# Loading slabs 2-3 in two halves of 64 partitions, slabs 4-5 in one piece, and the tables as 16 rows: a rotary embedding kernel

## The chip, the cores and the metric

The kernel runs on one core of a Trainium2 chip. The metric is the device time of one execution in microseconds. A core has TensorE (PE, matrix products), VectorE (DVE), ScalarE (ACT), GpSimd (POOL) and SyncE (SP), which run their own instruction streams and wait for one another by semaphores, and 16 DMA engines, which move data between the memory outside (HBM) and the core's own memory of 128 partitions. DMAs are issued here from SP (all loads of `x`) and from ACT (the tables and all stores), so there are two DMA queues, and every DMA engine has a ring of packets for each.

## The reference

```
x: [16, 512, 1024] f32, seen as [batch, seq, 16 heads, 64]; cos, sin: [512, 32] f32
x1, x2 = x[..., :32], x[..., 32:]
out = concatenate([x1 * cos - x2 * sin, x1 * sin + x2 * cos], axis=-1)
```

`cos` and `sin` depend on the place in the sequence alone: they are shared by all batches and heads. The input and the output have 33.55 MB each, the two tables 64 KB each.

## The kernel before, in words

The batch is cut into eight *slabs* of two batches (4.19 MB each). In a slab each of the 128 partitions holds 8 rows of 1024 numbers, 32 KB in one piece of HBM. Slabs 2-3 and 4-5 are *pairs*: there a partition holds 16 rows in sequence, 64 KB in one piece, and the first eight of them are called slab 2 or 4, the last eight slab 3 or 5. So a partition of a pair needs other rows of the tables than one of a single slab, and there are two sets of tables: `tab` for slabs 0, 1, 6, 7 and `tab2` for 2 to 5.

Loads are issued by SP in the order of the slabs, all at the start but for the last two: slab 0 and slab 1 (line 68), slabs 2-3 as one DMA of 128 packets of 64 KB (line 87), slabs 4 and 5 as two DMAs of 128 packets of 32 KB (line 90). The loads of slabs 6 and 7 take the memory of slabs 0 and 1 and wait until these are stored (line 68 again).

Work on a slab goes through ACT, DVE and ACT. ACT casts f32 to bf16 (`cast`, line 157), into the lower half of the slab's own memory. DVE makes two products with the tables (line 175) and a sum of one with the other shifted by half a head (line 176). ACT casts back to f32 (line 179) and issues the store. Slabs 0, 6 and 7 go through in two passes of 4096 columns, the others in one of 8192. The cast of the next pass is written ahead of the products of this one; within that, a scheduler fixes each engine's order when the kernel is built, and on the chip each engine keeps to it. Slabs 4 and 5 are stored by one DMA, the others by one each.

The tables are built at the start. `cos` and `sin` are loaded as 64 partitions of 1 KB (line 83), POOL casts them to bf16 (line 116), and PE spreads them over 128 partitions by products with 0/1/-1 matrices that POOL prepares (lines 94 to 109): four matmuls for `tab` (line 121, copied out of PSUM by DVE, line 127) and eight for `tab2` (line 133, copied by ACT, line 172). DVE's first product of slab 0 waits for `tab`.

Of the kernel before, what the change touches and what calls it, by code (L numbers as in the profile page):

```python
# [9 lines left out]
@with_exitstack  # L10
def kernel(
    ctx: ExitStack,
    tc: tile.TileContext,
    x: bass.AP,
    cos: bass.AP,
    sin: bass.AP,
    num_heads: int,
    out: bass.AP,
):
    nc = tc.nc  # L20
    P = nc.NUM_PARTITIONS

    batch, seq, dim = x.shape
    nh = num_heads
    hd = dim // nh
    half = hd // 2
    bf16 = mybir.dt.bfloat16
    f32 = mybir.dt.float32

    nb = 2  # L30
    nslabs = batch // nb
    rpp = nb * seq // P
    W = rpp * dim
    SP = seq // rpp
    TW = rpp * half

    out_flat = out.rearrange("b s h d -> b s (h d)")

    singles = ctx.enter_context(tc.tile_pool(name="singles", bufs=1))
    slabs = ctx.enter_context(tc.tile_pool(name="slabs", bufs=2))  # L40
    pairs = ctx.enter_context(tc.tile_pool(name="pairs", bufs=2))
    psum = ctx.enter_context(tc.tile_pool(
        name="psum", bufs=1, space=bass.MemoryType.PSUM))


    def dram(t, s, a=0, n=W):
        return bass.AP(tensor=t.tensor, offset=t.offset + s * nb * seq * dim + a,
                       ap=[[W, P], [1, n]])


    def view(t, offset, *dims):
        return dataclasses.replace(t, offset=t.offset + offset,
                                   ap=[t.ap[0], *[list(d) for d in dims]])

    slab = {}


    def paired(t, s, a=0, n=2 * W):
        return bass.AP(tensor=t.tensor, offset=t.offset + s * nb * seq * dim + a,
                       ap=[[2 * W, P], [1, n]])


    def load(s):
        slab[s] = slabs.tile([P, W], f32, tag="slab", name="slab")
        nc.sync.dma_start(out=slab[s], in_=dram(x, s))  # L68


    def place(s):
        t = pairs.tile([P, 2 * W], f32, tag="pair", name="pair")
        slab[s], slab[s + 1] = view(t, 0, (1, W)), view(t, W, (1, W))
        return t


    load(0)


    cos_sb = singles.tile([SP, TW], f32, tag="cos_sb")  # L80
    sin_sb = singles.tile([SP, TW], f32, tag="sin_sb")
    for t, src in ((cos_sb, cos), (sin_sb, sin)):
        nc.scalar.dma_start(out=t, in_=bass.AP(
            tensor=src.tensor, offset=src.offset, ap=[[TW, SP], [1, TW]]))

    load(1)
    nc.sync.dma_start(out=place(2), in_=paired(x, 2))
    pair = place(4)
    for h in range(2):
        nc.sync.dma_start(out=slab[4 + h], in_=paired(x, 4, h * W, W))  # L90


    pick = singles.tile([SP, 2 * P], bf16, tag="pick")
    nc.gpsimd.memset(pick, 0.0)  # L94
    for g in range(2):
        part = view(pick, g * P, (SP, P // SP), (1, SP))
        nc.gpsimd.affine_select(  # L97
            out=part, in_=part, compare_op=mybir.AluOpType.not_equal,
            fill=1.0 - 2.0 * g, base=0, pattern=[[0, P // SP], [-1, SP]],
            channel_multiplier=1)  # L100

    pick2 = singles.tile([SP, 4 * P], bf16, tag="pick2")
    nc.gpsimd.memset(pick2, 0.0)  # L105
    for h in range(2):
        for g in range(2):
            part = view(pick2, (2 * h + g) * P, (SP // 2, 2 * P // SP), (1, SP // 2))
            nc.gpsimd.affine_select(  # L109
                out=part, in_=part, compare_op=mybir.AluOpType.not_equal,  # L110
                fill=1.0 - 2.0 * g, base=-h, pattern=[[0, 2 * P // SP], [-2, SP // 2]],
                channel_multiplier=1)

    tab1 = singles.tile([SP, 2 * TW], bf16, tag="tab1")
    for i, t in enumerate((cos_sb, sin_sb)):
        nc.gpsimd.tensor_copy(out=view(tab1, i * TW, (1, TW)), in_=t)  # L116

    acc = psum.tile([P, 2 * rpp * hd], f32, tag="acc")
    for i in range(2):
        for h in range(2):  # L120
            nc.tensor.matmul(  # L121
                view(acc, i * rpp * hd + h * half, (hd, rpp), (1, half)),
                view(pick, i * h * P, (1, P)),
                view(tab1, i * TW, (half, rpp), (1, half)),
                start=True, stop=True)
    tab = singles.tile([P, 2 * rpp * hd], bf16, tag="tab")
    nc.vector.tensor_copy(out=tab, in_=acc)  # L127

    acc2 = psum.tile([P, 4 * rpp * hd], f32, tag="acc2")
    for i in range(2):  # L130
        for r in range(2):
            for h in range(2):
                nc.tensor.matmul(  # L133
                    view(acc2, (2 * i + r) * rpp * hd + h * half, (hd, rpp), (1, half)),
                    view(pick2, (2 * r + i * h) * P, (1, P)),
                    view(tab1, i * TW, (half, rpp), (1, half)),
                    start=True, stop=True)
    tab2 = singles.tile([P, 4 * rpp * hd], bf16, tag="tab2")

    passes = []
    for s in range(nslabs):
        n = rpp if 1 <= s < nslabs - 2 else rpp // 2
        passes += [(s, r, n) for r in range(0, rpp, n)]


    def halves(u):
        s, r, n = u  # L150
        t = view(slab[s], 0, (1, W)).bitcast(bf16)
        return [view(t, (2 * r + i * n) * dim, (1, n * dim)) for i in range(2)]


    def cast(u):
        s, r, n = u
        nc.scalar.copy(out=halves(u)[0], in_=view(slab[s], r * dim, (1, n * dim)))  # L157


    def factor(u, i):  # L160
        s, r, n = u
        t, a = (tab2, (2 * i + s % 2) * rpp * hd) if 2 <= s < 6 else (tab, i * rpp * hd)
        return view(t, a + r * hd, (hd, n), (0, nh), (1, hd))


    cast(passes[0])
    for i, u in enumerate(passes):
        s, r, n = u
        if i + 1 < len(passes):
            cast(passes[i + 1])  # L170
        if i == 0:
            tc.keep_in_program_order(nc.scalar.copy(out=tab2, in_=acc2))  # L172
        lo, up = halves(u)
        for k, t in enumerate((up, lo)):
            nc.vector.tensor_mul(out=t, in0=lo, in1=factor(u, k))  # L175
        nc.vector.tensor_add(  # L176
            out=up, in0=up, in1=view(lo, half, (hd, n * nh), (-half, 2), (1, half)))

        nc.scalar.copy(out=view(slab[s], r * dim, (1, n * dim)), in_=up)  # L179
        if r + n == rpp:  # L180
            if s == 5:
                nc.scalar.dma_start(out=paired(out_flat, 4), in_=pair)
            elif s in (2, 3):
                nc.scalar.dma_start(out=paired(out_flat, 2, (s - 2) * W, W), in_=slab[s])
            elif s != 4:
                nc.scalar.dma_start(out=dram(out_flat, s), in_=slab[s])
            if s < 2:
                load(s + 6)

# [34 lines left out]
```

## Time and profile before

| | |
|---|---|
| runs | 166.65 us median of 3 (164.38 to 167.47) |
| the profiled execution | 161.82 us, of which the span from first to last instruction is 160.0 us |
| DVE busy | 108.4 us (68%) |
| ACT busy | 115.1 us (72%) |
| PE, POOL busy | 2.9 and 3.3 us |
| DMA | 67.24 MB, mean 420 GB/s; packets 2176 |
| cosine, sine | landed 11.6 and 16.4 us after their issue |

The durations in the text come from the profiled execution, which is quicker than the median of the runs. A line of a table of groups or of the timeline names the source line, the engine, the operation, and the tiles written and read. Busy digits stand for slices of a fortieth of the span, 9 for 90% or more.

### The profile page before, as it was taken

To read this page: it belongs to the slowest core of one execution; us is meant where nothing else is said; L and a number is where in the kernel's file an instruction comes from. 1 tells how busy PE (TensorE), PEld (TensorE's weight loads), DVE (VectorE), ACT (ScalarE), POOL (GpSimd) and SP (SyncE) were. 2 spreads that over 40 slices of the span, in tenths; PEclk is the share of its full clock that TensorE was granted. 3 is DMA by queue.
4 is the path that set the end of the run, shared out by engine and by line. 5 is a ranking of instruction groups with operands and counts; after the bars stand their busy time and mean duration, and the time that the engine had idled before them with its cause. 6 is when DMAs were issued, how large, how long until landed. Compare 5 with 4: busy or idle time off the path is not lost.

```text
span 160.0 us, 179 instructions
## 1 busy us (share of the span) xinstructions
PE 2.9 (2%) x12; PEld 1.6 (1%) x12; DVE 108.4 (68%) x34; ACT 115.1 (72%) x24; POOL 3.3 (2%) x14
## 2 busy tenths in 40 slices
PE   0001410000000000000000000000000000000000
PEld 0000300000000000000000000000000000000000
DVE  0000299999971999899899989999279399910000
ACT  3005979994099999999999999399993999380000
POOL 6000000000000000000000000000000000000000
DMA  7999999699699999999999999999998998999994
GB/s 246 410 410 410 393 524 491 295 524 491 295 393 491 426 393 442 459 410 418 459 434 393 475 442 393 450 459 401 442 491 377 524 410 377 393 459 459 393 450 205
DMA packets 2176, 67.24 MB, mean 420 GB/s; under 512 B 256, under 2 KB 384, under 8 KB 384
## 3 DMA queue, kind: packets, MB, share of 16 engines
q1 hardware_dynamic: 1008, 33.55, 49.3%
q10 hardware_dynamic: 1168, 33.69, 48.8%
HBM read 33.69 MB, written 33.55 MB: 420 GB/s over the span
## 4 chain that ended last, share of the span: by engine, by line
DMA 67%; ACT 13%; issue 5%; DVE 4%; SPq 1%; ACTq 0%
DMA pair<-in_x_dram 27%; DMA slab<-in_x_dram 26%; DMA out_dram<-slab 15%; ACT slab L179 9%; DVE slab L175 3%; ACT slab L157 3%; ACT pair L157 2%; DVE slab L176 1%; SPq L68 1%; ACTq L179 0%; ACTq L157 0%
## 5 line engine op out<-in xcount | busy, mean ns | idle before, releaser
L175 DVE TENSOR_TENSOR slab<-slab,tab 128x4096 bf16<-128x4096 bf16 (+1 forms) x14 | 36.2, 2594 | 7.0 <-ACT slab L157 6.6
L157 ACT CAST slab<-slab 128x4096 bf16<-128x4096 f32 (+1 forms) x7 | 28.5, 4090 | 17.0 <-DMA slab<-in_x_dram 17.0
L175 DVE TENSOR_TENSOR pair<-pair,tab 128x8192 bf16<-128x8192 bf16 x8 | 35.4, 4424 | 6.2 <-ACT pair L157 6.0
L157 ACT CAST pair<-pair 128x8192 bf16<-128x8192 f32 x4 | 28.1, 7015 | 6.6 <-DMA pair<-in_x_dram 6.6
L179 ACT CAST slab<-slab 128x4096 f32<-128x4096 bf16 (+1 forms) x7 | 28.5, 4090 | 3.5 <-DVE slab L176 3.5
L179 ACT CAST pair<-pair 128x8192 f32<-128x8192 bf16 x4 | 28.1, 7016 | 0.3 <-DVE pair L176 0.3
L176 DVE TENSOR_TENSOR slab<-slab 128x4096 bf16<-128x4096 bf16 (+1 forms) x7 | 18.2, 2596 | 0.2
L176 DVE TENSOR_TENSOR pair<-pair 128x8192 bf16<-128x8192 bf16 x4 | 17.7, 4425 | 0.1
L127 DVE CAST tab<-acc 128x1024 bf16<-128x1024 f32 x1 | 1.2, 1224 | 18.8 <-PE acc L121 18.8
L157 ACT ACT_TABLE_LOAD x1 | 1.3, 1283 | 2.0 <-issue 2.0
L133 PE MATMUL acc<-tab,pick 64*128 64x256 bf16 x8 | 1.9, 414 | 0.0
L172 ACT CAST tab<-acc 128x2048 bf16<-128x2048 f32 x1 | 1.9, 1857 | 0.0
L121 PE MATMUL acc<-tab,pick 64*128 64x256 bf16 x4 | 1.2, 392 | 17.6 <-POOL tab L116 17.6
L133 PEld LDWEIGHTS <-pick 64*128 64x128 bf16 x8 | 1.1, 143 | 0.6
L109 POOL TENSOR_SCALAR_AFFINE_SELECT pick<-pick 64x128 bf16<-64x128 bf16 x4 | 1.1, 301 | 0.0
L121 PEld LDWEIGHTS <-pick 64*128 64x128 bf16 x4 | 0.5, 112 | 17.8 <-issue 15.9
L116 POOL CAST tab<-cos_sb 64x256 bf16<-64x256 f32 x1 | 0.4, 389 | 9.3 <-DMA cos_sb<-in_cos_dram 9.3
L97 POOL TENSOR_SCALAR_AFFINE_SELECT pick<-pick 64x128 bf16<-64x128 bf16 x2 | 0.5, 287 | 0.0
L105 POOL MEMSET pick<- 64x512 bf16 x1 | 0.5, 522 | 0.0
L116 POOL CAST tab<-sin_sb 64x256 bf16<-64x256 f32 x1 | 0.4, 394 | 4.9 <-DMA sin_sb<-in_sin_dram 4.9
L94 POOL MEMSET pick<- 64x256 bf16 x1 | 0.3, 304 | 0.3 <-POOLq L205 0.3
L205 POOL MEMSET const-bfloat16-1.0<- 128x1 bf16 x1 | 0.1, 111 | 0.0
(3 smaller groups left out, 0.3 us busy)
## 6 DMA issues: line engine op xcount, KB each, us to landing
slab<-in_x_dram SPq DMA_DIRECT2D x4, 4096.0 KB, 31.9
out_dram<-slab ACTq DMA_DIRECT2D x4, 4096.0 KB, 21.4
pair<-in_x_dram SPq DMA_DIRECT2D x2, 4096.0 KB, 71.0
out_dram<-pair ACTq DMA_DIRECT2D x2, 4096.0 KB, 31.8
cos_sb<-in_cos_dram ACTq DMA_DIRECT2D x1, 64.0 KB, 11.6
sin_sb<-in_sin_dram ACTq DMA_DIRECT2D x1, 64.0 KB, 16.4
pair<-in_x_dram SPq DMA_DIRECT2D x1, 42.7
out_dram<-pair ACTq DMA_DIRECT2D x1, 26.4
```

The costliest lines, as they stand in the source:

```text
L68: nc.sync.dma_start(out=slab[s], in_=dram(x, s))
L97: nc.gpsimd.affine_select(out=part, in_=part, compare_op=mybir.AluOpType.not_equal, fill=1.0 - 2.0 * g, base=0, pattern=[[0, P // SP], [-1 ...
L109: nc.gpsimd.affine_select(out=part, in_=part, compare_op=mybir.AluOpType.not_equal, fill=1.0 - 2.0 * g, base=-h, pattern=[[0, 2 * P // SP] ...
L116: nc.gpsimd.tensor_copy(out=view(tab1, i * TW, (1, TW)), in_=t)
L121: nc.tensor.matmul(view(acc, i * rpp * hd + h * half, (hd, rpp), (1, half)), view(pick, i * h * P, (1, P)), view(tab1, i * TW, (half, rpp) ...
L127: nc.vector.tensor_copy(out=tab, in_=acc)
L133: nc.tensor.matmul(view(acc2, (2 * i + r) * rpp * hd + h * half, (hd, rpp), (1, half)), view(pick2, (2 * r + i * h) * P, (1, P)), view(tab ...
L157: nc.scalar.copy(out=halves(u)[0], in_=view(slab[s], r * dim, (1, n * dim)))
L172: tc.keep_in_program_order(nc.scalar.copy(out=tab2, in_=acc2))
L175: nc.vector.tensor_mul(out=t, in0=lo, in1=factor(u, k))
L176: nc.vector.tensor_add(out=up, in0=up, in1=view(lo, half, (hd, n * nh), (-half, 2), (1, half)))
L179: nc.scalar.copy(out=view(slab[s], r * dim, (1, n * dim)), in_=up)
```

## The change

All pairs of slabs (0-1, 2-3, 4-5, 6-7) get the layout of 64 KB to a partition. Three pair tiles replace two slab tiles and two pair tiles; slabs 6-7 take the place of 0-1. Slabs 0, 1, 6 and 7 are still loaded and stored one by one, in packets of 32 KB. The tables are then the same for all pairs, and differ between even and odd slabs (`tabs[s % 2]`). `cos` and `sin` are loaded as 16 rows of 4 KB each into one tile of 128 partitions, which DVE sets to zero first, cosine at partitions 0, 8, 16, ..., sine at 4, 12, 20, ...; the matrices pick the rows, in pairs of accumulating matmuls.

```diff
-    slabs = ctx.enter_context(tc.tile_pool(name="slabs", bufs=2))
-    pairs = ctx.enter_context(tc.tile_pool(name="pairs", bufs=2))
+    pairs = ctx.enter_context(tc.tile_pool(name="pairs", bufs=3))
...
+    places = [pairs.tile([P, 2 * W], f32, tag="pair", name="pair") for _ in range(3)]
+    def here(s, n=1):
+        return view(places[s // 2 % 3], s % 2 * W, (1, n * W))
+    def there(t, s, n=1):
+        return bass.AP(tensor=t.tensor, offset=t.offset + s // 2 * 2 * P * W + s % 2 * W,
+                       ap=[[2 * W, P], [1, n * W]])
+    def load(s, n=1):
+        nc.sync.dma_start(out=here(s, n), in_=there(x, s, n))
+    def store(s, n=1):
+        nc.scalar.dma_start(out=there(out_flat, s, n), in_=here(s, n))
...
-    load(0)
-    cos_sb = singles.tile([SP, TW], f32, tag="cos_sb")
-    sin_sb = singles.tile([SP, TW], f32, tag="sin_sb")
-    for t, src in ((cos_sb, cos), (sin_sb, sin)):
-        nc.scalar.dma_start(out=t, in_=bass.AP(
-            tensor=src.tensor, offset=src.offset, ap=[[TW, SP], [1, TW]]))
-    load(1)
-    nc.sync.dma_start(out=place(2), in_=paired(x, 2))
-    pair = place(4)
-    for h in range(2):
-        nc.sync.dma_start(out=slab[4 + h], in_=paired(x, 4, h * W, W))
+    TR = 16
+    TC = seq * half // TR
+    raw = singles.tile([P, TC], f32, tag="raw")
+    nc.vector.memset(raw, 0.0)
+    load(0)
+    for i, src in enumerate((cos, sin)):
+        to = dataclasses.replace(
+            raw, offset=raw.offset + 4 * i * raw.ap[0][0],
+            ap=[[P // TR * raw.ap[0][0], TR], [1, TC]])
+        nc.scalar.dma_start(out=to, in_=bass.AP(
+            tensor=src.tensor, offset=src.offset, ap=[[TC, TR], [1, TC]]))
+    load(1)
+    for p in range(0, P, P // 2):
+        part = slice(p, p + P // 2)
+        nc.sync.dma_start(out=here(2, 2)[part], in_=there(x, 2, 2)[part])
+    load(4, 2)
...
+    pick = singles.tile([P, 6 * P], bf16, tag="pick")
+    nc.gpsimd.memset(pick, 0.0)
+    for g in range(3):
+        for m in range(2):
+            part = view(pick, (g * 2 + m) * P + m, (2 * TR, P // TR // 2), (2, TR))
             nc.gpsimd.affine_select(
                 out=part, in_=part, compare_op=mybir.AluOpType.not_equal,
+                fill=-1.0 if g == 2 else 1.0, base=-4 if g else 0,
+                pattern=[[0, P // TR // 2], [-(P // TR), TR]], channel_multiplier=1)
...
+    raw_b = singles.tile([P, TC], bf16, tag="raw_b")
+    nc.gpsimd.tensor_copy(out=raw_b, in_=raw)
+    accs, tabs = [], []
+    for h in range(2):
+        acc = psum.tile([P, 2 * rpp * hd], f32, tag=f"acc{h}", name="acc")
+        for g, at in ((0, 0), (0, half), (1, rpp * hd), (2, rpp * hd + half)):
+            for m in range(2):
+                nc.tensor.matmul(
+                    view(acc, at, (hd, rpp), (1, half)),
+                    view(pick, (g * 2 + m) * P, (1, P)),
+                    view(raw_b, (2 * m + h) * TW, (half, rpp), (1, half)),
+                    start=m == 0, stop=m == 1)
...
+    nc.vector.tensor_copy(out=tabs[0], in_=accs[0])
...
-            tc.keep_in_program_order(nc.scalar.copy(out=tab2, in_=acc2))
+            tc.keep_in_program_order(nc.scalar.copy(out=tabs[1], in_=accs[1]))
...
             if s == 5:
-                nc.scalar.dma_start(out=paired(out_flat, 4), in_=pair)
-            elif s in (2, 3):
-                nc.scalar.dma_start(out=paired(out_flat, 2, (s - 2) * W, W), in_=slab[s])
+                store(4, 2)
             elif s != 4:
-                nc.scalar.dma_start(out=dram(out_flat, s), in_=slab[s])
+                store(s)
```

The passes themselves are unchanged in the source. The order that the scheduler fixes for ACT and DVE is another one around slabs 1 to 3 (casts in are called "in", casts back "back"; DVE's two products of a slab are m and its sum a):

```
ACT before: ... 0 back, store 0, 2 in, 1 back, 3 in, store 1, 2 back, 4 in, store 2, 3 back, ...
ACT after:  ... 0 back, store 0, 1 back, store 1, 2 in, 3 in, 2 back, 4 in, store 2, 3 back, ...
DVE before: ... 1m 1m 1a, 2m 2m 2a, 3m 3m 3a, 4m ...
DVE after:  ... 1m 1m 1a, 2m 2m, 3m, 2a, 3m 3a, 4m ...
```

SP's order is that of the slabs in both. The load of slabs 4-5 now waits on the semaphore of load 0 before it is issued; the loads of slabs 6 and 7 wait for stores 0 and 1 as before.

More of the change, by code (lines that the diff above doesn't have):

```diff
@@ L33 @@
     W = rpp * dim
-    SP = seq // rpp
     TW = rpp * half
@@ L39 @@
     singles = ctx.enter_context(tc.tile_pool(name="singles", bufs=1))
-    slabs = ctx.enter_context(tc.tile_pool(name="slabs", bufs=2))
-    pairs = ctx.enter_context(tc.tile_pool(name="pairs", bufs=2))
+    pairs = ctx.enter_context(tc.tile_pool(name="pairs", bufs=3))
     psum = ctx.enter_context(tc.tile_pool(
         name="psum", bufs=1, space=bass.MemoryType.PSUM))
-    def dram(t, s, a=0, n=W):
-        return bass.AP(tensor=t.tensor, offset=t.offset + s * nb * seq * dim + a,
-                       ap=[[W, P], [1, n]])
     def view(t, offset, *dims):
@@ L53, in view @@
                                    ap=[t.ap[0], *[list(d) for d in dims]])
[L58 to L74, printed above, removed]
@@ L77 @@
-    load(0)
-    cos_sb = singles.tile([SP, TW], f32, tag="cos_sb")
-    sin_sb = singles.tile([SP, TW], f32, tag="sin_sb")
-    for t, src in ((cos_sb, cos), (sin_sb, sin)):
-        nc.scalar.dma_start(out=t, in_=bass.AP(
-            tensor=src.tensor, offset=src.offset, ap=[[TW, SP], [1, TW]]))
-    load(1)
-    nc.sync.dma_start(out=place(2), in_=paired(x, 2))
-    pair = place(4)
-    for h in range(2):
-        nc.sync.dma_start(out=slab[4 + h], in_=paired(x, 4, h * W, W))
-    pick = singles.tile([SP, 2 * P], bf16, tag="pick")
@@ L94 @@
-    nc.gpsimd.memset(pick, 0.0)
[L95 to L108, printed above, removed]
+    places = [pairs.tile([P, 2 * W], f32, tag="pair", name="pair") for _ in range(3)]
@@ L109 @@
+    load(4, 2)
+    pick = singles.tile([P, 6 * P], bf16, tag="pick")
+    nc.gpsimd.memset(pick, 0.0)
+    for g in range(3):
+        for m in range(2):
+            part = view(pick, (g * 2 + m) * P + m, (2 * TR, P // TR // 2), (2, TR))
             nc.gpsimd.affine_select(
                 out=part, in_=part, compare_op=mybir.AluOpType.not_equal,
-                fill=1.0 - 2.0 * g, base=-h, pattern=[[0, 2 * P // SP], [-2, SP // 2]],
-                channel_multiplier=1)
-    tab1 = singles.tile([SP, 2 * TW], bf16, tag="tab1")
@@ L115 @@
[L115 to L132, printed above, removed]
-                nc.tensor.matmul(
[L134 to L138, printed above, removed]
+                fill=-1.0 if g == 2 else 1.0, base=-4 if g else 0,
@@ new lines @@
+                pattern=[[0, P // TR // 2], [-(P // TR), TR]], channel_multiplier=1)
[6 more added lines that the diff above has]
+            for m in range(2):
+                nc.tensor.matmul(
+                    view(acc, at, (hd, rpp), (1, half)),
+                    view(pick, (g * 2 + m) * P, (1, P)),
+                    view(raw_b, (2 * m + h) * TW, (half, rpp), (1, half)),
+                    start=m == 0, stop=m == 1)
+        accs.append(acc)
+        tabs.append(singles.tile([P, 2 * rpp * hd], bf16, tag=f"tab{h}", name="tab"))
@@ L150, in halves @@
         s, r, n = u
-        t = view(slab[s], 0, (1, W)).bitcast(bf16)
+        t = here(s).bitcast(bf16)
         return [view(t, (2 * r + i * n) * dim, (1, n * dim)) for i in range(2)]
@@ L156, in cast @@
         s, r, n = u
[L157 to L163, printed above, removed]
+        nc.scalar.copy(out=halves(u)[0], in_=view(here(s), r * dim, (1, n * dim)))
     cast(passes[0])
@@ L171 @@
         if i == 0:
-            tc.keep_in_program_order(nc.scalar.copy(out=tab2, in_=acc2))
+            tc.keep_in_program_order(nc.scalar.copy(out=tabs[1], in_=accs[1]))
         lo, up = halves(u)
-        for k, t in enumerate((up, lo)):
-            nc.vector.tensor_mul(out=t, in0=lo, in1=factor(u, k))
+        for t, a in ((up, 0), (lo, rpp * hd)):
+            nc.vector.tensor_mul(
+                out=t, in0=lo,
+                in1=view(tabs[s % 2], a + r * hd, (hd, n), (0, nh), (1, hd)))
         nc.vector.tensor_add(
             out=up, in0=up, in1=view(lo, half, (hd, n * nh), (-half, 2), (1, half)))
-        nc.scalar.copy(out=view(slab[s], r * dim, (1, n * dim)), in_=up)
+        nc.scalar.copy(out=view(here(s), r * dim, (1, n * dim)), in_=up)
         if r + n == rpp:
             if s == 5:
-                nc.scalar.dma_start(out=paired(out_flat, 4), in_=pair)
-            elif s in (2, 3):
-                nc.scalar.dma_start(out=paired(out_flat, 2, (s - 2) * W, W), in_=slab[s])
+                store(4, 2)
             elif s != 4:
-                nc.scalar.dma_start(out=dram(out_flat, s), in_=slab[s])
+                store(s)
             if s < 2:
```

## The prediction

> **What bounds the kernel now.** I read the page's slices first, then the DMA share by stage, the timeline, the DMA view by window.
>
> ```profile
> span 160.0 us, 179 instructions
> ...
> DVE  0000299999971999899899989999279399910000
> ACT  3005979994099999999999999399993999380000
> ...
> DMA  7999999699699999999999999999998998999994
> ```
>
> The DMA row is full nearly throughout (a packet counts where it starts, hence some 6s). ScalarE (ACT) has a hole in the tenth and eleventh slices, VectorE (DVE) in the thirteenth, and both stand idle in the last four. The windows view gives share and rate by stage (columns: busy time per engine, clock, DMA share, GB/s):
>
> ```profile
> 22.00:42.00 20.00, 0.00 (x0) 0.00 (x0) 19.90 (x8) 14.75 (x4) 0.00 (x0) 1.00 0.98 423
> 44.00:118.00 74.00, 0.00 (x0) 0.00 (x0) 63.85 (x17) 70.67 (x12) 0.00 (x0) 1.00 1.00 432
> 120.00:138.00 18.00, 0.00 (x0) 0.00 (x0) 14.97 (x7) 14.66 (x5) 0.00 (x0) 1.00 1.00 433
> 140.00:157.00 17.00, 0.00 (x0) 0.00 (x0) 0.69 (x1) 3.60 (x1) 0.00 (x0) 1.00 1.01 436
> ```
>
> Loads alone (22 to 42), loads with stores, stores alone: about 432 GB/s each time. All 67.2 MB at that rate are 155.6 us of the 160.0. So the DMA engines are the bound, and compute only has to hand over the stores early enough. How much room it has, the timeline tells (start, duration, what, idle before it):
>
> ```profile
> 37.86 0.35 ACTq L186 DMA_DIRECT2D out_dram<-slab  x1
> 42.51 4.42 DVE L176 TENSOR_TENSOR slab<-slab 128x8192 bf16<-128x8192 bf16 x1
> 44.40 7.02 ACT L157 CAST pair<-pair 128x8192 bf16<-128x8192 f32 x1 [6.57 <-DMA pair<-in_x_dram]
> 51.33 7.01 ACT L179 CAST slab<-slab 128x8192 f32<-128x8192 bf16 x1
> 51.45 8.88 DVE L175 TENSOR_TENSOR pair<-pair,tab 128x8192 bf16<-128x8192 bf16 x2 [4.52 <-ACT pair L157]
> ...
> 113.45 0.34 ACTq L182 DMA_DIRECT2D out_dram<-pair  x1
> ...
> 144.41 0.34 ACTq L186 DMA_DIRECT2D out_dram<-slab  x1
> ```
>
> ACT takes slab 2's cast in as soon as it has landed (44.40), and only then casts slab 1 back (51.33). The last store is issued at 144.41, 15.6 us before the end, though 4.19 MB at 432 GB/s are 9.7 us: it queues behind earlier stores for 15.6 - 9.7 - 1.0 (issue to first packet) - 1.2 (last packet to the end) = 3.7 us. Compute that comes up to 3.7 us later costs nothing; beyond that each microsecond counts.
>
> **The change, part by part.**
>
> *64 KB descriptors for slabs 4-5.* The DMA view of three windows (6 to 16, 16 to 22, 124 to 136; packets, MB, share of 16 engines):
>
> ```profile
> q1 hardware_dynamic: 143, 4.16, 101.2%
> ...
> q1 hardware_dynamic: 79, 2.59, 100.2%
> ...
> q10 hardware_dynamic: 80, 5.24, 100.8%
> ```
>
> 79 packets of 32 KB in 6 us: 6 x 16 x 1.002 / 79 = 1.22 us each. 80 of 64 KB in 12 us: 12 x 16 x 1.008 / 80 = 2.42 us. Two small ones are 2.44, so 128 large for 256 small save 128 x 0.02 / 16 = 0.16 us in all. Packets of two queues take turns on an engine: cosine's four rounds of 1 KB need 11.6 us to land beside the loads. A 64 KB load packet against a 32 KB store packet then takes two thirds of the engine, so slabs 4-5 need 8 x (2.42 + 1.22) = 29 us and land at about 72. Slab 4 is wanted later than that (below, at C + 31.8). SP now waits for load 0 to land (13.3) before issuing this load; its ring then still holds the loads of slabs 1 to 3, so nothing runs dry.
>
> *Tables.* In the window from 6 to 16 us 127 load packets took 10 x 16 x 1.012 / 127 = 1.275 us instead of 1.22, because the 1 KB table packets land between them: 127 x 0.057 = 7.2 us, and 6.1 us of their own (3.8% of 10 x 16 us), so 13.3 / 16 = 0.8 us of DMA time. With 32 packets of the same bytes it is between a quarter of that and all of it: a gain of 0 to 0.6. Instead of five turns per table (four packets and a completion) there are two. Cosine is issued later, after a DVE memset of 128x1024 (not in the trace; between 0 and the 1.22 us of the 128x1024 copy out of PSUM; I take 1.2). First packets came at 6.0, so now 7.2; four turns of 1.3 make 12.4, and 0.5 until a waiting engine starts 12.9. POOL's cast of 128x1024: between 0.39 (the 64x256 row, if columns cost nothing) and 4 x 0.39 = 1.56; I take 1.4, to 14.3. Eight matmuls (eight took 1.91): 2.0, to 16.3. The copy to the table 1.2, to 17.5, as slab 0's first cast ends (17.4). DVE starts slab 0 at 17.5 instead of 20.13. POOL's longer memset and six selects lie under the 12 us of waiting; table 1's copy on ACT is 1.0 us instead of 1.86, in a hole before load 1 lands. If the tables came as late as before, everything below moves by 2.6.
>
> *The order on ACT and DVE.* This is what I price at most. ACT casts slab 1 back, issues store 1, and only then casts slab 2; DVE does slab 3's first multiply ahead of slab 2's add. DVE: slab 0 takes 6 x 2.29, slab 1 3 x 4.43, so 17.5 + 13.7 + 13.3 = 44.5. ACT casts slab 1 back from 44.5 to 51.5, having stood idle from 37.9. Slab 2's cast starts at C = 51.5, not 44.4, if slab 2 has landed. DVE is idle until C + 7.0.
>
> From C by program order, with 7.0 for an 8192 cast, 3.6 for a 4096 cast, 4.43 and 2.29 on DVE: slab 2's add is fourth on DVE and ends at C + 24.7; slab 2 back to C + 31.8, slab 4's cast to 38.9, slab 3 back to 45.9, slab 5's cast to 52.9; slab 5 on DVE from there to 66.2, back to 73.3, store 4-5 issued at C + 73.4 (before: 113.45 - 44.40 = 69.1). The four half passes then alternate ACT and DVE: store 6 at C + 87.6, store 7 at C + 101.7 (before: 100.0). So store 7 goes from 144.4 to 153.2, 8.8 later, against 3.7 of room. The end: store 4-5 finds the queue empty (store 2 is issued at C + 31.9 and store 3 at C + 46.0, 9.7 us of transfer each, so the engines stand idle before it), so C + 73.4 + 1.0 + 19.4 + 9.7 + 9.7 + 1.2 = C + 114.4 = 166 us. That is +6 without any price for the split.
>
> *Slabs 2-3 as two loads of 64 partitions.* One more DMA on SP, 0.45 us of issue, hidden under the ring. The two halves are in one ring, so one after the other on every engine, four 64 KB packets each.
>
> ```profile
> q1 hardware_dynamic: 1008, 33.55, 49.3%
> q10 hardware_dynamic: 1168, 33.69, 48.8%
> ```
>
> q10 holds 768 + 128 data packets of stores, 128 of the tables, and 1168 - 1024 = 144 = 9 x 16 completions: the tables, 64 partitions each, also ran on 16 engines. So will these halves. What a packet then costs, no row shows. Lower bound: 2.42 us, as over 128 partitions. Upper bound: everywhere in this trace 432 GB/s spread over 128 partitions, 3.4 GB/s for each; if that is what a partition's side takes, 64 of them take 216 GB/s, a packet 4.84 us, a half 19.4. The nearest row is the tables: 64 partitions, 16 engines, and the load packets beside them grew by 0.057 us although only 1 KB stood beside 32 KB. It is the one place where transfers cost more than their bytes, so I take the upper bound. Then: first half from 22.9 to 42.3; the second takes turns with store 0, whose packets start there: 4 x (4.84 + 1.22) = 24.2, to 66.5, and 0.5 until ACT starts. C = 67.0; the end at 67.0 + 114.4 = 181.4. Slabs 4-5 follow in the ring and land 29 us on, at 95.6, wanted at 98.8; loads 6 and 7, 19.4 us each beside stores, at 115 and 134.5, wanted at 126.9 and 147.4. None of them waits, though slab 4 only by 3 us. If the engines that share partitions fall out of step (one stores while the other loads), 4 x 4.84 gives C = 62.2 and 176.6.
>
> [...]
>
> *Sum.* Span 181.4, and 161.82 - 160.03 = 1.8 around it: 183.2 against 161.8 for the profiled execution. The median of the runs shown, 166.65, lies 4.8 above that execution; with the same distance 188.
>
> **Rivals.**
>
> *The split is free (the two halves run at full rate, or side by side).* Slab 2 has landed by 44, C = 51.5, end 166, with the same additions 172.6. For it: the 1 KB table packets themselves took only 6.1 / 128 = 0.047 us. Against: 1 KB says little of 64 KB. If the 4.8 us of the runs are slower transfers, they would hide part of the late compute and it is 170.
>
> *Not slower: the stores' backlog hides it.* Place: the queue ahead of store 7. If ACT and DVE come less than 3.7 us later, the DMA stays full and the time is that of the bytes: 160.0 - 0.6 - 0.2, in the runs about 166. For it: full DMA digits in every slice. Against: the program order, by which slab 2's cast cannot start before slab 1 is back, and this alone is 8.8. It decides at store 7's issue: up to 148 nothing is lost, after it everything.
>
> *The split costs part of it.* One engine of a sharing pair goes first each time and they get out of step: C between 55 and 62, ends of 170 to 177, runs of 176 to 183. It belongs to neither neighbour alone.
>
> **How the numbers follow.** The split at half rate, in step or nearly: 0.50 (runs 182 to 191, with late tables at the upper end). Part of the price: 0.12. Free split: 0.27. Not slower: 0.11. The likeliest gives 188. The range 169 to 192 holds the first three and leaves out the last. A measurement of this kernel tells about 2% from no change. Slower by over 2%: 0.50 + 0.12 + 0.24 of the free split = 0.86; within 2%: 0.03 + 0.09 = 0.12; faster: 0.02, since only 0.8 us of transfer time can be gained at all.
>
> **What would show it.** Right: slab 2's cast waits for a DMA until about 62 to 67; the DMA view between 24 and 40 shows about 216 GB/s at full share; DVE starts slab 0 near 17.5; store 1 is issued ahead of slab 2's cast; from that cast to store 7's issue 102 us; DMA digits below 9 between the fourth and fifth stores. Wrong: 430 GB/s between 24 and 40 and a cast of slab 2 at 51.5 (free split), or store 7 issued before 148 (no loss).

## The result, and the profile after

The changed kernel takes 183.75 us (median of 6 runs, 183.44 to 183.94). Against the kernel before on the same chip the ratio is 1.133, 95% interval 1.130 to 1.137: 13% slower. The profiled execution took 183.44 us with a span of 181.7 (before: 161.82 and 160.0). Some executions of the kernel before take 164 to 171 us, against near 162 for most; the ratio leaves them out, and the median shown at the start was of three such.

The page of the changed kernel, the rows that the prediction showed for the kernel before:

```profile
DVE  2004999998000000599999259989998299993000
ACT  2009869941930019990069999999759999965200
...
DMA  6999977999939989898999999999994999988995
```

DVE now stands idle from 44.6 to 74.7 us and ACT from 51.7 to 67.7 (the zeros from the eleventh and the thirteenth slice on), while the DMA engines are busy all the same (share 0.87 from 44 to 66, below). The other new thing is the 4 in the DMA row at 136 to 141 us: there the engines have nothing to do for part of the time (share 0.46). What the busy engines moved in the first idle stretch shows in the windows view (columns as before: stretch, busy times, clock, DMA share, GB/s):

```profile
24.00:40.00 16.00, 0.00 (x0) 0.00 (x0) 15.67 (x6) 14.03 (x3) 0.00 (x0) 0.50 0.96 197
44.00:66.00 22.00, 0.00 (x0) 0.00 (x0) 0.62 (x1) 7.02 (x1) 0.00 (x0) 0.50 0.87 243
68.00:96.00 28.00, 0.00 (x0) 0.00 (x0) 21.27 (x5) 17.25 (x3) 0.00 (x0) 0.50 0.99 429
```

From 24 to 40 only the first half of slabs 2-3 is being loaded: share 0.96, and 197 GB/s where the kernel before had 423 (22 to 42 us). Sixteen engines at 0.96 that move 197 GB/s need 16 x 0.96 x 65.5 KB / 197 GB/s = 5.1 us for a packet of 64 KB, against 2.42. The second half shares the engines with store 0 (44 to 66: 243 GB/s in all). Once the load of slabs 4-5, over 128 partitions, has its turn (68 to 96), the rate is 429 again.

The timeline of the changed kernel at the places that the prediction named:

```profile
17.47 6.82 DVE L148 TENSOR_TENSOR pair<-pair,tab 128x4096 bf16<-128x4096 bf16 x3 [0.67 <-ACT pair L136]
...
51.70 0.34 ACTq L68 DMA_DIRECT2D out_dram<-pair  x1
67.65 13.94 ACT L136 CAST pair<-pair 128x8192 bf16<-128x8192 f32 x2 [15.98 <-DMA pair<-in_x_dram]
74.70 13.22 DVE L148 TENSOR_TENSOR pair<-pair,tab 128x8192 bf16<-128x8192 bf16 x3 [30.08 <-ACT pair L136]
...
140.63 0.34 ACTq L68 DMA_DIRECT2D out_dram<-pair  x1
...
168.99 0.34 ACTq L68 DMA_DIRECT2D out_dram<-pair  x1
```

DVE starts slab 0 at 17.47, when its cast is there (the table has been since 16.8). Store 1 is issued at 51.70, and then ACT waits 15.98 us for slab 2: C, the start of its cast, is 67.65. Store 4-5 is issued at C + 73.0, store 7 at C + 101.3, and the span ends at C + 114.0. DVE waits 30.08 us for that cast.

### The profile page after: what moved, and what is told of

The parts are those of the page before. It is cut to its first block, busy times and chain, and to the rows that moved or that the text cites. A ratio compares the mean times of both kernels' runs of the same rounds, so it can differ in the third digit from the quotient of the medians.

```text
span 181.7 us, 187 instructions
## 1 busy us (share of the span) xinstructions
PE 3.6 (2%) x16; PEld 2.3 (1%) x16; DVE 109.1 (60%) x35; ACT 114.3 (63%) x24; POOL 3.3 (2%) x12
## 4 chain that ended last, share of the span: by engine, by line
ACT 33%; DVE 28%; DMA 13%; issue 9%; another core or an unknown queue 9%; ACTq 0%; SPq 0%
DVE pair L148 20%; ACT pair L154 18%; ACT pair L136 16%; DMA pair<-in_x_dram 13%; DVE pair L151 9%; SPq L64 0%; ACTq L68 0%; ACTq L154 0%; ACTq L136 0%
## 5 line engine op out<-in xcount | busy, mean ns | idle before, releaser
L148 DVE TENSOR_TENSOR pair<-pair,tab 128x4096 bf16<-128x4096 bf16 (+1 forms) x22 | 71.6, 3260 | 41.2 <-ACT pair L136 40.8
L136 ACT CAST pair<-pair 128x4096 bf16<-128x4096 f32 (+1 forms) x11 | 56.5, 5153 | 27.7 <-DMA pair<-in_x_dram 27.7
L154 ACT CAST pair<-pair 128x4096 f32<-128x4096 bf16 (+1 forms) x11 | 56.6, 5154 | 23.8 <-DVE pair L151 23.7
L151 DVE TENSOR_TENSOR pair<-pair 128x4096 bf16<-128x4096 bf16 (+1 forms) x11 | 35.9, 3260 | 0.3
L110 PE MATMUL acc<-raw_b,pick 128*128 128x256 bf16 x16 | 3.6, 414 | 13.7 <-POOL raw_b L103 13.7
L110 PEld LDWEIGHTS <-pick 128*128 128x128 bf16 x16 | 2.3, 142 | 14.5 <-issue 11.7
L75 DVE MEMSET raw<- 128x1024 f32 x1 | 0.9, 912 | 1.0 <-PEq L178 1.0
L97 POOL TENSOR_SCALAR_AFFINE_SELECT pick<-pick 128x64 bf16<-128x64 bf16 x6 | 1.3, 263 | 0.1
L103 POOL CAST raw_b<-raw 128x1024 bf16<-128x1024 f32 x1 | 1.0, 1037 | 9.7 <-DMA raw<-in_sin_dram 9.7
L145 ACT CAST tab<-acc 128x1024 bf16<-128x1024 f32 x1 | 1.0, 1004 | 0.0
```

What stands on the lines that cost most here:

```text
L75: nc.vector.memset(raw, 0.0)
L97: nc.gpsimd.affine_select(out=part, in_=part, compare_op=mybir.AluOpType.not_equal, fill=-1.0 if g == 2 else 1.0, base=-4 if g else 0, pat ...
L103: nc.gpsimd.tensor_copy(out=raw_b, in_=raw)
L110: nc.tensor.matmul(view(acc, at, (hd, rpp), (1, half)), view(pick, (g * 2 + m) * P, (1, P)), view(raw_b, (2 * m + h) * TW, (half, rpp), (1 ...
L136: nc.scalar.copy(out=halves(u)[0], in_=view(here(s), r * dim, (1, n * dim)))
L145: tc.keep_in_program_order(nc.scalar.copy(out=tabs[1], in_=accs[1]))
```

## The experiments

Two theories stood against each other after this. The first: the price lies in which partitions the two halves are (a property of the shape), plus the order that the scheduler took up with the split. The second: any transfer of 64 partitions is slow, or the second load costs something in itself, or tables, layout and the loads of slabs 4-5 have a part in it. The expectations below name their own theories A and B, each for its experiment.

### Even and odd partitions instead of lower and upper half

```diff
-    for p in range(0, P, P // 2):
-        part = slice(p, p + P // 2)
+    for p in range(2):
+        part = slice(p, P, 2)
         nc.sync.dma_start(out=here(2, 2)[part], in_=there(x, 2, 2)[part])
```

> The changed kernel with its two loads of slabs 2-3 cut by even and odd partitions instead of lower and upper half; the program order on ACT and DVE is that of the changed kernel. Theory A (what costs is which partitions a transfer reaches, and even ones reach as much of the memory's side as all do): packets of 64 KB take 2.42 us as over 128 partitions, 24 to 40 us runs at about 430 GB/s, slab 2 has landed by 44, its cast starts when slab 1 is back, at 51.7, and the span is 51.7 + 114.0 (the changed kernel's way from this cast to its end, 181.65 - 67.65) = 165.7, time 167.5. Theory B (a transfer of 64 partitions is slow as such, whichever they are): 5.1 us a packet, 197 GB/s from 24 to 40, cast at 67.6, span 181.7, time 183.5. [...]

Measured: 167.6 us, ratio to the kernel before 1.032 (1.028 to 1.037), span 165.8. The windows of this run, over the first half's time and over the gap before store 4-5 (issued at 124.79):

```profile
24.00:40.00 16.00, 0.00 (x0) 0.00 (x0) 15.90 (x7) 13.58 (x3) 0.00 (x0) 0.50 1.08 459
118.00:126.00 8.00, 0.00 (x0) 0.00 (x0) 6.44 (x3) 8.00 (x2) 0.00 (x0) 0.50 0.46 197
```

A packet counts where it starts, so a share above 1 is the window's edge; 459 / 1.08 = 425 GB/s. The transfers of 64 partitions run at full rate when they are every second partition. That is theory A, and its number (165.7) came out too. What is left, 5.4 us over the unsplit kernel below, is the order: the DMA engines are busy 0.46 of the time from 118 to 126, because store 4-5 comes too late.

### Slabs 2-3 in one load

```diff
-    for p in range(0, P, P // 2):
-        part = slice(p, p + P // 2)
-        nc.sync.dma_start(out=here(2, 2)[part], in_=there(x, 2, 2)[part])
+    load(2, 2)
```

> The changed kernel with slabs 2-3 in one load of 128 partitions; with that the order on ACT and DVE is the one of the kernel before (slab 2 in, then slab 1 back). Theory A (the loss is the split's packets plus the order that comes with it; layout, 64 KB loads of slabs 4-5 and tables cost nothing): slab 2's cast at 44, store 7 issued near 144, DMA share near 1.00 throughout, span 159.2 to 160, time 161 to 162. Rival (part of the loss sits in the tables, the zeroed tile or the loads of slabs 4-5): slab 4 waits for its load, or slab 0 starts after 20, and the span is above 163.

Measured: 161.81 us, ratio 0.998 (0.996 to 1.001), span 160.4. Its timeline at slab 2's cast:

```profile
44.67 7.02 ACT L134 CAST pair<-pair 128x8192 bf16<-128x8192 f32 x1 [7.22 <-DMA pair<-in_x_dram]
51.59 7.01 ACT L152 CAST pair<-pair 128x8192 f32<-128x8192 bf16 x1
```

Slab 2 goes in at 44.67, ahead of slab 1 back at 51.59: with one load the scheduler builds the old order by itself. The whole loss is gone. So layout, tables and the 64 KB loads of slabs 4-5 together cost nothing, and together they gain nothing that can be measured either (they were not tried one by one): DVE starts slab 0 2.8 us earlier, at 17.35, but the DMA engines are the bound: their share is 1.08 from 24 to 40 us, 0.99 from 96 to 118, 1.05 from 110 to 126 and 0.98 from 126 to 156, at 426 to 459 GB/s.

### The split halves in the old order

```diff
-        nc.scalar.copy(out=view(here(s), r * dim, (1, n * dim)), in_=up)
+        back = nc.scalar.copy(out=view(here(s), r * dim, (1, n * dim)), in_=up)
+        if s in (1, 2):
+            tc.keep_in_program_order(back)
```

> The changed kernel with its two half loads, but with slab 1's cast back pinned behind slab 2's cast on ACT (the order of the kernel before). Theory A (half loads and order are not a sum: the packets lengthen the DMA work, the order leaves DMA idle): slab 2's cast at 67.6, slab 1 back only at 81.6; store 7 issued at 67.6 + 100 = 168; DMA work is 157 us of the kernel before plus 128 packets x 2.4 us more / 16 = 19, so with 1.7 before it and 1.2 behind it at least 178.9 if it never stands idle: span 178 to 180, time 180 to 182. Rival (they add up): 181.7 - 6 = 175.7, time 177.5.

Measured: 181.77 us, ratio 1.120 (1.114 to 1.125), span 180.1. The old order gives back only 1.6 us of the 21.7 when the halves stay: its DMA row has no gap.

```profile
DMA  6999999999929969989899999999999999989994
```

(The 2 is a slice in which few of the long packets start: 87 GB/s in the page's row, with 335 and 284 beside it.) The two causes are not a sum. The long packets make the DMA work longer. They took 5.1 us in the first half and, beside store 0, 4.47 in the second (lines under "The split" below), against 2.42: 64 x 2.68 + 64 x 2.05 = 303 us more, 19 on each of 16 engines. By this estimate the span is about 179 without a gap; 180.1 was measured. The order makes the DMA engines wait, but with the halves less than without: 1.6 us of span here, 5.4 above. Slab 2's cast and store 4-5 in this run:

```profile
68.20 7.02 ACT L136 CAST pair<-pair 128x8192 bf16<-128x8192 f32 x1 [30.29 <-DMA pair<-in_x_dram]
...
137.30 0.34 ACTq L68 DMA_DIRECT2D out_dram<-pair  x1
```

In both kernels slab 2's cast starts when its load lands (68.20 here, 67.65 in the changed kernel): there, slab 1's cast back lies in a wait and delays nothing. What is left of the order is store 4-5, 3.3 us earlier here (137.30 against 140.63).

### Transfers alone, in ten shapes

One tile, loaded and stored in shapes one after the other, one execution; the casts, products and sums are left out:

```
    whole = [slice(0, P)]
    halves = [slice(0, 64), slice(64, P)]
    evenodd = [slice(0, P, 2), slice(1, P, 2)]
    quarters = [slice(p, p + 32) for p in range(0, P, 32)]
    combs = [slice(p, P, 4) for p in range(4)]
    ...
    for part in halves:
        sync.dma_start(out=tile_[part], in_=there(x, 1)[part])
    ...
    for eng, part in zip((sync, act), halves):
        eng.dma_start(out=tile_[part], in_=there(x, 1)[part])
    ...
```

> Transfers alone, no computation (casts, products and sums are left out; the output is copies of the input): 8.39 MB in packets of 64 KB into one tile, each stage after the one before: all 128 partitions; lower and upper half; even and odd; four runs of 32; four combs of every fourth partition; the two halves at once on two queues; then stores of all, halves, even and odd, four runs. Theory A (the lower and the upper 64 partitions, and within each half every run of 32, reach half of the memory's side): 19.4 us for all, 41 for halves, 19.4 for even and odd, 41 for runs of 32, 19.4 for combs. Theory B (each partition takes at most 3.2 GB/s): 19.4, 41, 41, 82, 82. At once on two queues: 41 if the engines keep in step, down to 19.4 if not. Stores: as the loads if the limit is in the memory's side for reading too, 19.4 for all shapes if it is only in writing it.

Measured, in its timeline (each load stage is issued when the one before has landed, so the distance of two lines is the time of a stage; 8.39 MB at the 432 GB/s seen below are 19.4 us, so some 2.6 us of the first are issue and landing):

```profile
0.73 0.39 SPq L55 DMA_DIRECT2D pair<-in_x_dram  x1
22.75 1.18 SPq L57 DMA_DIRECT2D pair<-in_x_dram  x2
66.03 1.13 SPq L59 DMA_DIRECT2D pair<-in_x_dram  x2
88.34 1.73 SPq L61 DMA_DIRECT2D pair<-in_x_dram  x4
131.12 2.39 SPq L63 DMA_DIRECT2D pair<-in_x_dram  x4
153.37 0.49 SPq L65 DMA_DIRECT2D pair<-in_x_dram  x1
153.55 0.56 ACTq L65 DMA_DIRECT2D pair<-in_x_dram  x1
195.83 0.36 ACTq L67 DMA_DIRECT2D out_dram<-pair  x1
```

All 128 partitions: 22.0 us. Lower and upper half: 43.3. Even and odd: 22.3. Four runs of 32: 42.8. Four combs of every fourth: 22.3. The two halves at once on two queues: 42.5. The times of theory A hold for every load, with packets of about 5.1 us in the runs (from 96 to 128 the windows view has a share of 0.96 and 197 GB/s: 16 x 0.96 x 65.5 KB / 197 GB/s). That such a run reaches half of the memory's side was the author's explanation; the runs show the times alone. Theory B falls: 32 partitions in a run are as quick as 64 in a run (42.8 and 43.3 us), and 32 spread out twice as quick (22.3).

A half is also one piece of 4.19 MB of HBM, while even or odd partitions take every second 64 KB. The kernel before speaks against this as the cause: slab 1 is such a piece too, goes to all 128 partitions, and its packets take 1.22 us for 32 KB, the full rate (431 GB/s from 16 to 22 us).

Two queues at once are no way around it. The DMA view of two stretches of that stage (163 to 168, 168 to 173) shows why: all sixteen engines take a packet of the lower half from SP's queue (q1), then all sixteen one of the upper half from ACT's (q10), 5 x 16 x 0.989 / 16 = 4.9 us each. They keep in step there, so only one half is served at a time; over 160 to 192 the rate is 203 GB/s at a share of 0.96.

```profile
q1 hardware_dynamic: 16, 1.05, 98.9%
...
q10 hardware_dynamic: 16, 1.05, 98.9%
```

The stores followed one another without a wait, and the windows view gives their rate (all, halves, even and odd, runs of 32):

```profile
198.00:215.00 17.00, 0.00 (x0) 1.00 1.00 432
218.00:254.00 36.00, 0.00 (x0) 1.00 0.99 204
262.00:274.00 12.00, 0.00 (x0) 1.00 1.01 437
284.00:314.00 30.00, 0.00 (x0) 1.00 0.95 208
```

Stores, which read the core's memory, are halved by the same shapes as loads, which write it: 204 and 208 GB/s against 432 and 437.

### Even and odd, in the old order

The even and odd loads of the first experiment with the pin of the third.

> Even and odd partitions as two loads, and slab 1's cast back pinned behind slab 2's cast in, as in the kernel before. Theory A (two loads instead of one cost nothing in themselves): the unsplit kernel again, span 160 to 161, slab 2's cast near 44.5. Rival (the second load in the ring or its wait costs something of its own): slab 2's cast past 46, span above 162.

Measured: 162.03 us, ratio 0.999 (0.997 to 1.000), span 160.1. Slab 2's cast and store 4-5:

```profile
44.39 7.02 ACT L136 CAST pair<-pair 128x8192 bf16<-128x8192 f32 x1 [6.88 <-DMA pair<-in_x_dram]
...
114.61 0.34 ACTq L68 DMA_DIRECT2D out_dram<-pair  x1
```

Two loads for one cost nothing in themselves (span 160.1 against 160.4 with one). (This run and the next are from another chip than the four before; the kernel before takes near 162 us on both.)

### Which of the two orders it is

The even and odd loads again, ACT in the changed order, and on DVE alone the old one:

```diff
-            nc.vector.tensor_mul(
+            product = nc.vector.tensor_mul(
                 out=t, in0=lo,
                 in1=view(tabs[s % 2], a + r * hd, (hd, n), (0, nh), (1, hd)))
+            if s == 3:
+                tc.keep_in_program_order(product)
```

> Even and odd partitions as two loads, ACT in the order of the changed kernel (slab 1 back and store 1 ahead of slab 2's cast), but slab 3's first product pinned behind slab 2's sum on DVE. If DVE's order is the larger part of the 5.4 us that the two orders together cost: slab 2 starts at C = 51.8, its sum ends at C + 20.3 instead of C + 24.7, store 4-5 is issued at C + 68.8 = 120.6 and store 7 at C + 97.2 = 149.0, and the span is at most 120.6 + 1.0 + 38.8 + 1.2 = 161.6, at least the 160.4 of the full DMA. If ACT's order alone costs it: span 165 or more, as with both.

Measured: 163.38 us, ratio 1.008 (1.005 to 1.011), span 161.5. The first line is the store of slabs 4-5 in the first experiment, with both orders changed, the second in this one:

```profile
124.79 0.34 ACTq L68 DMA_DIRECT2D out_dram<-pair  x1
```

```profile
120.49 0.34 ACTq L68 DMA_DIRECT2D out_dram<-pair  x1
```

4.3 us earlier, one product of DVE, and the span is shorter by just that. Of the 5.7 us between this pair of orders and the old ones (165.8 against 160.1), slab 3's product ahead of slab 2's sum makes 4.3, and slab 1 back ahead of slab 2 in makes 1.4. (The 1.4 is small but clear: all six times of this kernel lie above all ten of the one before it. DVE's order alone, with ACT's old one, was not tried.) The DMA share ahead of store 4-5 tells the same: 0.46 from 118 to 126 with both orders, 0.76 with ACT's alone.

```profile
118.00:126.00 8.00, 0.00 (x0) 0.00 (x0) 4.21 (x2) 8.00 (x3) 0.00 (x0) 0.50 0.76 328
```

## Why the prediction was right

*What bounds it.* Right: with the packets at full rate and the old order (the unsplit kernel) the time is that of the bytes (161.81 us against near 162).

*64 KB loads of slabs 4-5.* Priced at 0.16 us of gain, and nothing can be seen of it. The turns of the two queues held (from 44 to 62 in the changed kernel each had 48 packets): in the unsplit kernel slab 4's cast waits 0.96 us for its load and starts at 73.41, so it landed at about 73 (72 was forecast).

*Tables.* Start of slab 0 at 17.47, forecast 17.5. Each term was taken a little too large: memset 0.91 (1.2 taken), the waiting POOL started 12.58 (12.9), POOL's cast 1.04 (1.4 taken), eight matmuls 1.9 (2.0). So the table was there at 16.8 instead of 17.5, and the start came out only because slab 0's first cast ends at 17.4 and DVE needs that too. The early start did not matter in the changed kernel, where C is set by the load of slabs 2-3.

*The order.* The walk from C held within 0.5 us: store 4-5 at C + 73.0 (73.4), store 7 at C + 101.3 (101.7), the end at C + 114.0 (114.4). The price without the split, 166, came out as 165.8 with even and odd partitions. But the text put the blame on ACT ("this alone is 8.8"); the last experiment shows that ACT's part of it costs 1.4 us and DVE's 4.3. The room of 3.7 us at the last store was not the whole rule either: with ACT's order alone store 7 is issued at 148.84, 4.4 us later than before, and the span is 1.5 us longer where 0.7 would follow from that room, because the engines run short of work ahead of store 4-5 already (share 0.76 from 118 to 126).

*The split.* The upper bound was the right one to take, but its reason was wrong, so its number came out by luck. The prediction derived it from a cap of each partition, and by that cap even and odd partitions would have been as slow as halves, and runs of 32 twice as slow; the ones run at full rate (22.3 us), the others take the same as halves (42.8 against 43.3). No run shows such a cap. The shapes show 425 to 437 GB/s, or a little less than half of that (197 for the first half's load, 204 and 208 for the stores of halves and of runs of 32), and nothing between; no run shows why. Two errors lie in the sum, one each way. The first half's packets took 5.1 us instead of 4.84, 5% more; why the rate is a little below half is open. The second half beside store 0 went quicker than taken. The DMA view from 44 to 62 (18 us):

```profile
q1 hardware_dynamic: 48, 3.15, 74.5%
q10 hardware_dynamic: 48, 1.57, 23.0%
```

That is 18 x 16 x 0.745 / 48 = 4.47 us for a load packet and 1.38 for a store packet, together 5.85 where 4.84 + 1.22 = 6.06 were taken. The two nearly cancel: C came to 67.65 against 67.0.

*A table row that proved nothing.* The load packets beside the 1 KB table packets had grown from 1.22 to 1.275, and the prediction called this the nearest sign of a price for 64 partitions. With 16 rows of 4 KB they grow as much: in the changed kernel 128 packets of 32 KB in the same window (144 less 16 completions) take 10 x 16 x 1.016 / 128 = 1.27 us.

```profile
q1 hardware_dynamic: 144, 4.19, 101.6%
```

Rows at every eighth partition slow the loads as rows at 64 partitions in a run did, so the growth was no sign of what such a run costs, and the gain of the new tables in DMA time is near the lower end of the 0 to 0.6.

*The last term.* Span 181.4 forecast, 181.7 measured; 183.2 forecast for the profiled execution, 183.44 measured. The 4.8 us on top, the distance of the earlier median to its profiled execution, was the term that was wrong: it is 0.3 in the changed kernel (183.75 against 183.44). With it the forecast was 188.

*The rivals.* The free split fell (197 GB/s from 24 to 40), and so did the split that costs a part: C came at 67.65, past its range of 55 to 62; the sharing pairs that it speaks of, no trace shows. "Not slower" fell with store 7 at 169.

## What to carry to other kernels

When a transfer is cut by partitions, what counts is which ones: here, with packets of 64 KB, a run of 64 or 32 about halved the rate of all sixteen engines, for loads (43.3 and 42.8 us for 8.39 MB against 22.0) and stores (204 and 208 GB/s against 432), while loads over every second or every fourth partition (22.3 us each) and stores over every second (437 GB/s) kept it. A cut of a load also changes what the scheduler does with the work behind it, so compare the instruction order of every engine before the time; one product of DVE in another place cost 4.3 us here. And where the DMA engines are full, an earlier start of compute (2.8 us here) was worth nothing, and a delay cost only the time for which it left the engines without work (1.5 us, for a last store 4.4 us later).

## What the hardware showed that was not expected

The granted TensorE clock over the span reads near 0.56 in some executions and 1.0 in others, of one and the same kernel: in the unsplit kernel 0.56 in seven of twelve, with even and odd loads in the old order in three of ten. All six executions of the changed kernel read 0.56, and every recorded one of the kernel before 1.0. The times do not follow it: the unsplit kernel took 161.57 to 162.22 us at 0.56 and 161.59 to 162.17 at 1.0, the split halves in the old order 181.67 and 181.70 at 0.56 and 181.65 to 181.91 at 1.0. TensorE's last matmul ends at 20.5 us in the kernel before and at 17.2 in the changed one. Why the clock differs was not tried.

Two queues with a half each were hardly faster than one queue with both (42.5 against 43.3 us), although each engine had packets for both halves at hand: the engines took them in step, as shown above (16 packets of one queue from 163 to 168, 16 of the other from 168 to 173).
